# Attention outputs and blended tiles are split as they come, and one more feed-forward tile is computed plainly

## The chip, the cores and the metric

One Trainium2 chip, one core. The time is device microseconds of one execution. The kernel runs alone on its core; there are no collectives.

## What is computed

One inference step of a two-layer backbone for two groups of tokens that share all weights: 128 context tokens and 512 latent tokens, 640 in all, model width 1024. Cut to what the change touches, each layer is:

```python
h = rms_norm(x) * (1 + scale1) + shift1
z = h @ w_in                                  # conv streams, q, k, v, S5 input, three gates
y_attn = block_attention(q, k, v)             # 16 heads, 4 key/value heads
merged = sigmoid(g_conv) * (y_conv @ w_proj_conv) \
       + sigmoid(g_attn) * (y_attn @ w_proj_attn) \
       + sigmoid(g_ssm) * (y_ssm @ w_proj_ssm)
x = x + gate1 * (merged @ w_out)
h = rms_norm(x) * (1 + scale2) + shift2
x = x + gate2 * ((silu(h @ w_ffn_gate) * (h @ w_ffn_up)) @ w_ffn_down)   # width 2816
```

Scale, shift and gate come from an adaLN product with w_ada. All of it is float32 in and out.

## The kernel before

Activations lie transposed: a tile (`c2`) holds 128 channels of all 640 tokens, so a width of 1024 is 8 tiles. To keep float32 precision, each operand of a large product is split in a high half (a cast on ScalarE, to fp32r) and a low half (a subtraction on VectorE); `split` (L257) does it for activations and `halves` (L426) for weights. A product is then three terms, high-high, high-low and low-high, in two halves of 320 tokens: six matmuls of 320 columns for each of 8 k-tiles, 48 for an output tile (`gemm`, L844; `tile_gemm`, L982). `gemm` takes the k-tiles in order, so its matmuls wait for the split tiles one after the other.

Weights go through a ring of three raw tiles (`wr`), filled by DMAs on SP's queue in the order in which they are used, and three split tiles (`wh`). A converter runs at most two units ahead of the unit in use (`may`, L423). An adaLN unit (raw weights, no split) counts as one of these. `ada_n` (L319) says how many follow which tile: two after projection tile 0 ("pa", m=0), one after each of the others. What isn't converted when `w_get` (L488) asks for it is issued then, behind everything issued so far.

The program is written out by hand in one order for all engines. The main line is a generator (`layer`, L1895); beside it run side generators, for the attention seven of them. `pump` (L538) decides by a clock of its own, kept in Python while the program is written, which step comes next: a side step whose inputs are ready by the time the main line could go on is issued first. Each engine then runs its instructions in the order in which they were issued.

The attention works in four blocks b of four heads. `attn_out` (L1344) adds the outputs of block b into the two tiles ya[2b] and ya[2b+1]: eight products over the latent tokens (n = 0 to 7), then one over the context (n = 8), so both tiles of a block are complete only after its last product. While attention runs, the main line computes, in this order, q projections, gates, the GLU and the S5 branch, and the last gates (`gates`, L1934). Then `drain(att)` (L1946) issues the rest of the attention with nothing from the main line in between. All 8 ya tiles are split, and the projection runs: 8 tiles "pa", each evacuated by `blend` (L1017), two VectorE operations that multiply with the gate and add into merged[m]. After the eighth, all 8 merged tiles are split (L1952), x is reloaded from DRAM on SP's queue, and the 8 output tiles "o" follow, with `finish_x` (L1958) as evacuation.

PSUM has four tiles of two banks (`psb`). The pool of `c2` tiles has 57 (`NTILES`, L45). Counted in the program's order, from the first write of a tile to its last read, the most in use at once is 56, early in block b=2 of either layer.

The feed forward has 22 tiles of width 128 in five parts (`FF_PARTS`: 4, 4, 4, 5, 5). For each tile it needs a gate and an up product. Tiles below `PLAIN` take 2 x 48 matmuls. Those from `PLAIN` on are pairs (`glu_pair`, L906): a Strassen-Winograd scheme of seven quarter products, 7 x 12 = 84 matmuls, with sums of the weights made by two accumulating DMAs on POOL's queue and VectorE additions, and sums of h made by the side `sums` (L865) during the first tiles and by `quarters` (L890), which runs once, before the first pair. It makes four casts and four subtractions, half a tile wide each. After the tiles of a part comes its share of the down projection, 8 tiles of 24 matmuls (in the first four-tile part 192 in all), each added to x on VectorE by `gated`.

Of the kernel before, what the change touches and what calls it, by code (L numbers as in the profile page):

```python
# [17 lines left out]
KD = D // 128  # L18
# [13 lines left out]
GO = 0  # L32
# [13 lines left out]
WH = 3  # L46
RES = 1
FF_PARTS = ((0, 4), (4, 4), (8, 4), (12, 5), (17, 5))
PLAIN = 3
KS = (0, 4, 1, 5, 2, 6, 3, 7)  # L50
GQ = 4
GE = GQ * NCH
# [117 lines left out]
def trunk_kernel(ctx: ExitStack, tc: tile.TileContext, a):  # L170
    nc = tc.nc
    clk = Clock()
    pe, act, dve, sp, pool = (Engine(e, k, clk) for e, k in (
        (nc.tensor, "pe"), (nc.scalar, "act"), (nc.vector, "dve"), (nc.sync, "dma"), (nc.gpsimd, "pool")))
# [10 lines left out]
    def c2(dt=F32):  # L185
        return tp.tile([128, TK], dt, tag="c2", name="c2")
# [12 lines left out]
    def gps():  # L199
        t = bps()  # L200
        clk.held.add(t.name)
        clk.spare = 0
        return t

    def release(*ps):
        for t in ps:
            clk.held.discard(t.name)
# [7 lines left out]
    def f32(x):  # L215
        return x.bitcast(F32)
# [4 lines left out]
    def tt(out, in0, in1, op):  # L221
        dve.tensor_tensor(out=out, in0=in0, in1=in1, op=op)
# [4 lines left out]
    def add(out, x, y):  # L227
        tt(out, x, y, OP.add)

    def sub(out, x, y):  # L230
        tt(out, x, y, OP.subtract)
# [25 lines left out]
    def split(x):  # L257

        hi, lo = c2(F32R), c2(F32R)
        act.copy(hi, x)  # L260
        sub(lo, x, f32(hi))
        return hi, lo
# [56 lines left out]
    def ada_n(key):  # L319

        nm, l, m = key
        if nm == "pa":
            return 1 + int(m == 0)
        if nm == "fgu":
            return int(l == 0 and m < 14)
        if nm == "fd":
            return int(l == 0 and m in (4, 8))
        return int(nm == "o" and m < 7 - GO or l == 0 and (nm in ("cc", "cb") or nm == "fg" and m > 1))

    def tblk(key, *args):  # L330
        wblk(key, *args)
        ada_blk(ada_n(key))

    for l in range(DEPTH):
# [33 lines left out]
        for r0, nr in FF_PARTS:  # L368
            for m in range(r0, r0 + nr):
                if m < PLAIN:  # L370
                    tblk(("fg", l, m), a["w_ffn_gate"][l], 0, KD, 128 * m, 128)
# [116 lines left out]
    def w_get(key):  # L488
        u = wst["use"]
        assert units[u] == key, (units[u], key)  # L490
        wst["use"] += 1
        wst["used"] += 1 - wst["over"]
        wst["over"] = int(key[0] == "fgu" and key[3] == 3)
        while u not in wtile:
            cvt.step()
        return wtile.pop(u)
# [41 lines left out]
    def pump(need=(), until=None):  # L538

        own = [x for x in need if isinstance(x, str) and x in clk.t]  # L540
        m = clk.ready(need)
        while until is None or not until.done:
            if until is not None:
                m = INF
            elif not own:
                m = max(clk.ready(need), clk.t["pe"])
            t, x = min(((x.time(), x) for x in sides if not x.busy and not (x.prio == -1 and wst["hold"]) and (x.prio < 0 or not clk.calm)), key=lambda y: y[0], default=(INF, None))
            if t > m + SLACK or x is None or own and t == m and x.prio >= 0:
                return
            assert t < INF  # L550
            x.step()

    def drain(side):
        clk.spare = 0
        pump(until=side)
# [118 lines left out]
    def ada_pre(n):  # L674

        for l, v, q, kh in ada_gaps[:n]:
            w = []
            for j in range(2):
                t = c2()[:, 0:512].rearrange("p (k m) -> p k m", k=2)
                r0, c0 = 512 * kh + 256 * j, v * D + q * 256  # L680
                sp.dma_start(t, a["w_ada"][l][r0:r0 + 256, c0:c0 + 256].rearrange("(k p) m -> p k m", p=128))
                w += [t[:, 0, :], t[:, 1, :]]
            ada_w.append(w)
        del ada_gaps[:n]
# [159 lines left out]
    def gemm(ps, w, c0, acts, first=True, last=True, ks=None):  # L844

        K = len(acts)
        for i, k in enumerate(ks or range(K)):
            x = acts[k]
            if last and i >= K - RES:
                clk.spare = 1  # L850
            yield (w[0],) + x + (() if i else (ps,))
            for n, (r, s) in enumerate(((0, 0), (0, 1), (1, 0))):
                for h in range(2):
                    mm(ps[:, h, 0:HN], w[r][:, k, c0:c0 + 128], x[s][:, h * HN:(h + 1) * HN],
                       first and i == 0 and n == 0, last and i == K - 1 and n == 2)
# [116 lines left out]
    def v2(t):  # L972
        return t.rearrange("p (h n) -> p h n", h=2)
# [8 lines left out]
    def tile_gemm(key, acts, evac):  # L982
        w = w_get(key)
        ps = gps()
        yield from gemm(ps, w, 0, acts)
        evac(ps)
        release(ps)
        for _ in range(ada_n(key)):
            yield from ada_step()
# [27 lines left out]
    def blend(merged, m, th, ps):  # L1017

        stt(v2(th), v2(th), 1.0, pv2(ps), OP.add, OP.mult)
        if len(merged) <= m:  # L1020
            merged.append(th)
        else:
            add(merged[m], merged[m], th)
# [125 lines left out]
    class Attn:  # L1149
        pass  # L1150

    def attn_kv(l, A):
        A.cache = c2()
        for i, nm in enumerate(("cache_k", "cache_v")):
            sp.dma_start(A.cache[:, 256 * i:256 * i + 256], a[nm][0, l].rearrange("t h d -> t (h d)"))
        attn_tables(l)
        A.k, A.v = [], []
        yield from token_major(("k", l), A.hs, A.k)
# [182 lines left out]
            if PT:  # L1341
                pts.append(PT)

    def attn_out(preps, pts, done, ya):  # L1344

        for b in range(4):
            for n in range(9):
                yield lambda: len(pts) > done[4]
                vs, kp = preps[b][5], preps[b][4]
                PT = pts[done[4]]  # L1350
                yield PT[1], "b"
                ps = bps()
                if n < 8:
                    w = 256
                    prods = [(vs[:, 128 * k:128 * k + 128], PT[r][:, :, 128 * k:128 * k + 128])
                             for k in range(5) for r in range(2)]
                else:
                    w = 512
                    prods = [(kp[:, 256:384], PT[r][:, 0, 0:512]) for r in range(2)]
                for k, (v, p) in enumerate(prods):  # L1360
                    mm(ps[:, 0, 0:w], v, p, k == 0, k == len(prods) - 1)
                pts[done[4]] = None
                done[4] += 1
                clk.held.add(ps.name)
                yield ps, "act"
                u = c2()[0:64, 0:w]
                act.copy(u, ps[64:128, 0, 0:w])
                yield u,
                release(ps)
                if n < 8:  # L1370
                    r, c = 64 * (n // 2 % 2), 128 + 256 * (n % 2)
                    add(ya[2 * b + n // 4][r:r + 64, c:c + 256], ps[0:64, 0, 0:256], u)
                else:
                    for h in range(4):
                        r, c = 64 * (h % 2), slice(128 * h, 128 * h + 128)
                        add(ya[2 * b + h // 2][r:r + 64, 0:128], ps[0:64, 0, c], u[:, c])

    def attn_begin(l, A, raws, ya):
        preps, scores, exps, probs, turned, pts, done = [], [], [], [], [], [], [0] * 5
        out = Side(attn_out(preps, pts, done, ya), 0)  # L1380
        Side(attn_split(turned, pts, done), 0.1)
        Side(attn_turn(probs, turned, done), 0.2)
        Side(attn_norm(exps, probs), 0.5)
        Side(attn_exp(scores, exps), 0.7)
        Side(attn_scores(preps, scores, exps, done), 1)
        Side(attn_prep(l, A, raws, preps, done), 2)
        return out
# [507 lines left out]
    def layer(l, xs, stat, ssm):  # L1895
        up, ysT = ssm[1:]
        ssm = ssm[0]
        yc, merged = [], []
# [10 lines left out]
        merged = []  # L1909
        if l + 1 < DEPTH:  # L1910
            place_vecs(l + 1)
        A = Attn()
        A.hs, A.after = hs, ssm[1]
        yield from attn_kv(l, A)
        raws = []
# [3 lines left out]
            yield from token_major(("q", l, b), hs, raw)  # L1919
            raws.append(raw)  # L1920

        ya = [c2() for _ in range(KD)]
        att = attn_begin(l, A, raws, ya)
        v = []
        yield from token_major(("v", l), hs, v)
        A.v = v
# [5 lines left out]
        ths = []  # L1932
# [10 lines left out]
        ys = yield from glu(l, ysT)  # L1943
        yield from branch(l, "gs", "ps", hs, ys, merged)
        yield from gates(GA + GB, KD)
        drain(att)  # L1946
        ya = [split(y) for y in ya]
        for m in range(KD):
            yield from tile_gemm(("pa", l, m), ya, lambda ps: blend(merged, m, ths[m], ps))
            if m >= 8 - GO:  # L1950
                ada_pre(1)
        ms = [split(y) for y in merged]  # L1952
        ada_flush(l, 2)
        xs = reload_x()
        stat = []
# [20 lines left out]
        for part, (m0, nm) in enumerate(FF_PARTS):  # L1976
            hid = []
            tail = iter([0, 0, 0])
            for m in range(m0, m0 + nm):
                if m >= PLAIN:  # L1980
                    if x is None:
# [36 lines left out]
            for m in range(KD):  # L2018
# [4 lines left out]
                if m < 2:  # L2023
                    if m == 0:
                        two = yield from pair_ps(("fd", l, 0, m0), ("fd", l, 1, m0), hid)
                    ps = two[m]
                else:
                    ps = gps()
# [144 lines left out]
```

## Time and profile before

| | us |
|---|---|
| median of 3 runs | 2593.35 |
| lowest and highest | 2589.13, 2595.61 |
| the profiled execution | 2593.81 |
| its span | 2591.8 |

The profile is of one execution. Engines are PE (TensorE's matmuls), PEld (its weight loads, which overlap the matmuls), DVE (VectorE), ACT (ScalarE), POOL and SP (whose queue issues most DMAs). A matmul's recorded duration includes the time until its result has left the array, so matmuls of a stream overlap in the record; the pace is read from many of them in a row. All instructions are issued by one helper (L132), so rows are told apart by tiles: c is any activation tile, wh split weights, wr raw weights, pt the attention's probabilities or the pairs' weights, bps PSUM, ident the identity of a transpose. "[1.30 <-ACT c L132]" is the engine's idle time just before the instruction, and what ended it.

### The profile page before, as it was taken

Reading aid. Unit: us, or ns where it says so; the run is one execution under the profiler, and the core shown is the slowest. Engines: PE = TensorE matmul, PEld = TensorE weight load, DVE = VectorE, ACT = ScalarE, POOL = GpSimd, SP = SyncE. Lnnn points to the kernel's source line nnn. Section 1 sums busy time; section 2 is a strip of 40 time slices with the busy share of each in tenths; the row PEclk is TensorE's granted clock in tenths of the full one; section 3 lists DMA queues with packets and bytes.
Section 4 is the critical chain, followed back from the end, with each engine's and each line's share of the span. In section 5 each row is a group of like instructions: output and inputs, shape, how many; then the busy total and the mean of one; then the engine's idle time right before and its main releaser. Section 6 shows DMA issues by size and latency. Waiting matters only on the chain. (4 is left out here: it accounts for less than half of the span.)

```text
span 2591.8 us, 45359 instructions
## 1 busy us (share of the span) xinstructions
PE 2494.3 (96%) x18235; PEld 2398.9 (93%) x18235; DVE 1838.0 (71%) x3502; ACT 1155.5 (45%) x2096; POOL 97.9 (4%) x80
## 2 busy tenths in 40 slices
PE   6999999999999999999989999999998999999998
PEld 4899999999888899999979999899997889999998
DVE  5888787788744666675678887777887447766665
ACT  4343336556722533443443333365666225433443
POOL 0000000000000010111000000000000000111110
PEclk8999999999999999999989999999999999999999
DMA  9433331221037366665553233212110572565552
GB/s 267 139 106 114 96 96 51 64 67 42 17 114 237 92 144 141 147 145 128 122 167 94 78 99 117 63 44 86 52 45 24 175 201 58 118 143 123 114 125 72
DMA packets 465202, 280.46 MB, mean 108 GB/s; under 512 B 60184, under 2 KB 453216, under 8 KB 464992
## 3 DMA queue, kind: packets, MB, share of 16 engines
q1 hardware_dynamic: 424864, 257.63, 34.2%
q0 software_dynamic: 40128, 19.93, 6.2%
q8 instruction: 144, 2.36, 0.4%
q14 instruction: 66, 0.54, 0.1%
HBM read 257.37 MB, written 20.12 MB: 107 GB/s over the span
## 5 line engine op out<-in xcount | busy, mean ns | idle before, releaser
L132 PE MATMUL bps<-c,wh 128*128 128x320 f32 x11760 | 1822.7, 313 | 42.0 <-ACT c L132 20.7
L132 PEld LDWEIGHTS bps<-c,wh 128*128 128x128 f32 x11760 | 1745.3, 189 | 77.5 <-ACT c L132 25.8
L132 DVE TENSOR_TENSOR c<-c,c 128x512 f32<-128x512 f32 (+8 forms) x750 | 423.8, 592 | 57.9 <-ACT c L132 47.8
L132 ACT CAST wh<-wr 128x1024 fp32r<-128x1024 f32 (+2 forms) x286 | 267.9, 940 | 315.6 <-PE bps L132 157.7
L132 DVE TENSOR_TENSOR wh<-wr,wh 128x1024 fp32r<-128x1024 f32 (+2 forms) x286 | 309.3, 1086 | 129.7 <-ACT wh L132 128.6
L132 ACT COPY c<-bps 128x320 f32<-128x320 f32 (+7 forms) x363 | 150.7, 437 | 255.5 <-PE bps L132 250.8
L132 PE MATMUL bps<-c,c 128*128 128x320 f32 (+2 forms) x1416 | 234.8, 303 | 10.1 <-DVE c L132 6.5
L132 PEld LDWEIGHTS bps<-c,c 128*128 128x128 f32 x1416 | 204.4, 191 | 15.1 <-ACT c L132 10.4
L132 DVE TENSOR_TENSOR c<-c,bps 128x320 f32<-128x320 f32 (+1 forms) x222 | 125.0, 564 | 122.2 <-ACT c L132 106.4
L132 ACT ACTIVATE c<-c 128x640 f32<-128x640 f32 (+4 forms) x131 | 93.5, 722 | 210.2 <-DVE c L132 210.0
L132 PE MATMUL bps<-wh,c 128*128 128x256 f32 x1440 | 183.7, 286 | 2.9 <-ACT c L132 2.7
L132 PE MATMUL bps<-ident,c 128*128 128x128 f32 (+1 forms) x1115 | 159.2, 279 | 23.8 <-DVE c L132 9.9
L132 PEld LDWEIGHTS bps<-wh,c 128*128 128x128 f32 x1440 | 177.4, 193 | 3.8 <-ACT c L132 3.3
L132 ACT CAST c<-c 128x640 fp32r<-128x640 f32 (+3 forms) x192 | 113.4, 619 | 117.9 <-DVE c L132 116.8
L132 PEld LDWEIGHTS bps<-ident,c 128*128 128x128 f32 (+1 forms) x1115 | 131.1, 144 | 35.9 <-issue 10.2
L132 DVE SCALAR_TENSOR_TENSOR c<-bps,g2T,c 128x128 f32<-128x128 f32 (+2 forms) x240 | 89.7, 433 | 84.6 <-PE bps L132 84.6
L132 POOL DMA_DIRECT2D pt<-in_w_ffn_gate_dram x38 | 48.9, 1287 | 2344.8 <-DMA pt<-in_w_ffn_up_dram 2018.6
L132 DVE SCALAR_TENSOR_TENSOR c<-c,c 128x640 f32<-128x640 f32 (+3 forms) x124 | 102.8, 836 | 47.2 <-ACT c L132 45.4
L132 ACT ACTIVATE c<-bps,mx 128x640 f32<-128x640 f32 (+1 forms) x160 | 113.3, 712 | 36.4 <-DVE mx L132 35.7
L132 DVE TENSOR_REDUCE mx<-bps 128x1 f32<-128x640 f32 (+1 forms) x136 | 109.6, 809 | 27.8 <-PE bps L132 27.2
L132 ACT CAST wh<-pt 128x1024 fp32r<-128x1024 f32 x76 | 79.9, 1051 | 84.9 <-PE bps L132 83.7
L132 DVE TENSOR_TENSOR pt<-bps,pt 128x640 fp32r<-128x640 f32 (+1 forms) x136 | 109.4, 810 | 9.9 <-ACT pt L132 8.9
(105 smaller groups left out, 1541.2 us busy)
## 6 DMA issues: line engine op xcount, KB each, us to landing
wr<-in_w_in_dram SPq DMA_DIRECT2D x104, 512.0 KB
c<-in_w_ada_dram SPq DMA_DIRECT2D x110, 256.0 KB
wr<-in_w_ffn_gate_dram SPq DMA_DIRECT2D x44, 512.0 KB
wr<-in_w_ada_dram SPq DMA_DIRECT2D x41, 512.0 KB
pt<-in_w_ffn_up_dram SPq DMA_DIRECT2D x38, 512.0 KB
wr<-in_w_ffn_down_dram SPq DMA_DIRECT2D x48, 256.0 KB
wr<-in_w_ffn_down_dram SPq DMA_DIRECT2D x32, 320.0 KB
pt<-in_w_ffn_up_dram SPq DMA_DIRECT2D x38, 256.0 KB
```

Of the source, the lines that this page charges most:

```text
L132: res = f(*args, **kw)
```

## The change

`attn_out` splits the two tiles of a block as soon as the block is complete, and appends the halves to a list `yas`. This list, of the new class `Late`, says that it has 8 entries; when an entry is asked for that isn't there, the side generators are run until it is. `drain(att)` is gone: the projection begins at once, and `gemm` asks for one k-tile after the other. Each merged tile is split right after its own projection tile. `pump` takes a condition as well as a side to wait for. The `ada_pre` call that is dropped did nothing (GO is 0). `PLAIN` goes from 3 to 4: tile m=3 is computed plainly in both layers, so the whole first part is, and the first pair (and with it `quarters`) is m=4, after the first part's down projection.

```diff
--- before.py
+++ after.py
@@ -46,7 +46,7 @@
 WH = 3
 RES = 1
 FF_PARTS = ((0, 4), (4, 4), (8, 4), (12, 5), (17, 5))
-PLAIN = 3
+PLAIN = 4
 KS = (0, 4, 1, 5, 2, 6, 3, 7)
 GQ = 4
 GE = GQ * NCH
@@ -539,7 +539,8 @@
 
         own = [x for x in need if isinstance(x, str) and x in clk.t]
         m = clk.ready(need)
-        while until is None or not until.done:
+        over = (lambda: False) if until is None else until if callable(until) else lambda: until.done
+        while not over():
             if until is not None:
                 m = INF
             elif not own:
@@ -1148,6 +1149,19 @@
 
     class Attn:
         pass
+
+    class Late(list):
+
+
+        def __len__(self):
+            return KD
+
+        def __getitem__(self, k):
+            n = list.__len__
+            if n(self) <= k:
+                clk.spare = 0
+                pump(until=lambda: n(self) > k)
+            return list.__getitem__(self, k)
 
     def attn_kv(l, A):
         A.cache = c2()
@@ -1341,7 +1355,7 @@
             if PT:
                 pts.append(PT)
 
-    def attn_out(preps, pts, done, ya):
+    def attn_out(preps, pts, done, ya, yas):
 
         for b in range(4):
             for n in range(9):
@@ -1374,10 +1388,13 @@
                     for h in range(4):
                         r, c = 64 * (h % 2), slice(128 * h, 128 * h + 128)
                         add(ya[2 * b + h // 2][r:r + 64, 0:128], ps[0:64, 0, c], u[:, c])
-
-    def attn_begin(l, A, raws, ya):
+            for y in ya[2 * b:2 * b + 2]:
+                yield y, "act"
+                yas.append(split(y))
+
+    def attn_begin(l, A, raws, ya, yas):
         preps, scores, exps, probs, turned, pts, done = [], [], [], [], [], [], [0] * 5
-        out = Side(attn_out(preps, pts, done, ya), 0)
+        out = Side(attn_out(preps, pts, done, ya, yas), 0)
         Side(attn_split(turned, pts, done), 0.1)
         Side(attn_turn(probs, turned, done), 0.2)
         Side(attn_norm(exps, probs), 0.5)
@@ -1919,8 +1936,8 @@
             yield from token_major(("q", l, b), hs, raw)
             raws.append(raw)
 
-        ya = [c2() for _ in range(KD)]
-        att = attn_begin(l, A, raws, ya)
+        ya, yas = [c2() for _ in range(KD)], Late()
+        att = attn_begin(l, A, raws, ya, yas)
         v = []
         yield from token_major(("v", l), hs, v)
         A.v = v
@@ -1943,13 +1960,11 @@
         ys = yield from glu(l, ysT)
         yield from branch(l, "gs", "ps", hs, ys, merged)
         yield from gates(GA + GB, KD)
-        drain(att)
-        ya = [split(y) for y in ya]
+        ms = []
         for m in range(KD):
-            yield from tile_gemm(("pa", l, m), ya, lambda ps: blend(merged, m, ths[m], ps))
-            if m >= 8 - GO:
-                ada_pre(1)
-        ms = [split(y) for y in merged]
+            yield from tile_gemm(("pa", l, m), yas, lambda ps: blend(merged, m, ths[m], ps))
+            ms.append(split(merged[m]))
+            merged[m] = None
         ada_flush(l, 2)
         xs = reload_x()
         stat = []
```

## Rows read from the trace of the kernel before

**Rows 1.** Section 1 of the page: busy us, share of the span, instructions.

```profile
PE 2494.3 (96%) x18235; PEld 2398.9 (93%) x18235; DVE 1838.0 (71%) x3502; ACT 1155.5 (45%) x2096; POOL 97.9 (4%) x80
```

**Rows 2.** Who TensorE waited for, whole span: us in total, times, longest.

```profile
PE bps L132 <- DVE c L132: 33.6, 39, 4.2
```

**Rows 3.** Stretches: us, busy time of each engine (instructions), granted clock, DMA.

```profile
584.00:600.00 16.00, 16.00 (x117) 15.56 (x116) 11.76 (x24) 11.27 (x22) 0.00 (x0) 1.00 0.12 35
693.00:718.00 25.00, 18.69 (x120) 15.65 (x118) 19.18 (x40) 18.91 (x42) 0.00 (x0) 0.93 0.00 1
718.00:728.00 10.00, 9.42 (x62) 8.71 (x62) 6.49 (x9) 4.41 (x7) 0.00 (x0) 0.83 0.00 0
1937.00:1968.00 31.00, 31.00 (x230) 30.37 (x229) 21.12 (x43) 21.48 (x44) 0.00 (x0) 1.00 0.06 18
1968.00:1995.00 27.00, 20.93 (x145) 17.53 (x143) 22.63 (x46) 20.22 (x47) 0.00 (x0) 1.00 0.00 1
```

**Rows 4.** TensorE by line and shape, 1937 to 1968: busy us, mean ns, idle before.

```profile
L132 PE MATMUL bps<-c,wh 128*128 128x320 f32 x108 | 18.5, 314 | 0.0
```

**Rows 5.** Timeline, layer 0: start, us, engine, form, count, idle before.

```profile
716.48 1.19 DVE L132 TENSOR_TENSOR c<-bps,c 64x128 f32<-64x128 f32 x4 [0.41 <-ACT c L132]
...
718.58 8.55 PE L132 MATMUL bps<-c,wh 128*128 128x320 f32 x46 [0.90 <-DVE c L132]
...
727.06 1.07 PE L132 MATMUL bps<-wr,csT 128*32 128x256 f32 x16
```

**Rows 6.** Timeline, the same place in layer 1.

```profile
1993.92 5.12 ACT L132 CAST c<-c 128x640 fp32r<-128x640 f32 x8
1994.05 1.19 DVE L132 TENSOR_TENSOR c<-bps,c 64x128 f32<-64x128 f32 x4 [0.26 <-ACT c L132]
...
1996.16 7.01 PE L132 MATMUL bps<-c,wh 128*128 128x320 f32 x46 [0.90 <-DVE c L132]
...
2003.09 1.07 PE L132 MATMUL bps<-wr,csT 128*32 128x256 f32 x16
```

**Rows 7.** Timeline, projection tiles 0 to 2 of layer 0.

```profile
728.02 0.82 DVE L132 TENSOR_TENSOR c<-c,c 128x640 f32<-128x640 f32 x1
...
730.04 6.72 PE L132 MATMUL bps<-c,wh 128*128 128x320 f32 x44 [1.12 <-DVE wh L132]
...
737.26 7.30 PE L132 MATMUL bps<-c,wh 128*128 128x320 f32 x48
```

**Rows 8.** Timeline, first output tile: layer 0, then layer 1.

```profile
784.07 0.55 PE L132 MATMUL bps<-c,wh 128*128 128x320 f32 x2
...
786.08 7.01 PE L132 MATMUL bps<-c,wh 128*128 128x320 f32 x46 [1.46 <-DVE c L132]
...
2062.11 7.01 PE L132 MATMUL bps<-c,wh 128*128 128x320 f32 x46 [1.46 <-DVE c L132]
```

**Rows 9.** Timeline, feed forward m=2 and m=3: layer 0, then layer 1.

```profile
897.29 10.82 PE L132 MATMUL bps<-c,wh 128*128 128x320 f32 x72
...
922.20 0.64 PE L132 MATMUL bps<-c,csT 128*32 128x256 f32 x8
...
2178.74 4.56 PE L132 MATMUL bps<-c,wh 128*128 128x320 f32 x30
...
2180.68 3.42 ACT L132 CAST c<-c 128x640 fp32r<-128x640 f32 x7 [3.85 <-DVE c L132]
...
2185.42 2.65 PE L132 MATMUL bps<-c,wh 128*128 128x320 f32 x12 [2.12 <-ACT c L132]
...
2196.17 4.56 PE L132 MATMUL bps<-c,wh 128*128 128x320 f32 x30
```

**Rows 10.** Timeline, layer 1: down projection of part 0 and pair m=4.

```profile
2201.63 34.56 PE L132 MATMUL bps<-c,wh 128*128 128x320 f32 x234
...
2225.71 1.05 ACT L132 CAST wh<-pt 128x1024 fp32r<-128x1024 f32 x1 [2.47 <-PE bps L132]
2226.80 1.23 DVE L132 TENSOR_TENSOR wh<-pt,wh 128x1024 fp32r<-128x1024 f32 x1
```

## The prediction

> **What bounds the kernel now.** I read the busy shares first: TensorE is busy in 96% of the span [rows 1]. Then the list of who TensorE waited for; its longest entry, VectorE, is 33.6 us in all [rows 2]. So a change gains by fewer matmuls or in the gaps near the edited lines, and those I looked up. The table of stretches shows the first: while gates run beside the attention, TensorE is busy 31.00 of 31 us; when the gates have run out it is busy 18.69 of 25 us in layer 0 and 20.93 of 27 in layer 1, a tail that is a chain through VectorE (22.63 of 27) and ScalarE [rows 3]. The timelines show the others: projection 0 limping behind the splits of the attention outputs [rows 5, 6], projection 1 waiting for weights [rows 7], a wait in the first output tile [rows 8], a stall at the first Strassen pair, m=3 [rows 9]. The sum is made against the profiled execution, 2593.81 us (the span 2591.8 and 2.0 around it); the median shown is 0.46 lower, and I carry the difference over to it.
>
> **Pace.** 234 matmuls of 320 columns without a gap take 34.56 us [rows 10], 0.148 each; that price holds for all of them below. The Trainium skill, "TensorE: Matmul & The Clock Gate", section "Back-to-back issue gap", gives N/2.4 + 2.5 ns for an isolated matmul at full clock, 0.136 us here; by it the 24 matmuls that are added below would cost an estimated 3.3 us, not 3.6. The row decides.
>
> **Projection 0.** In layer 0 the attention's last additions end at 716.48 + 1.19 = 717.67, and the work after projection 0 starts at 727.06: 9.4 us [rows 5]. In layer 1 it is 1994.05 + 1.19 = 1995.24 to 2003.09, 7.85 us [rows 6]. The difference is the clock: 46 matmuls take 8.55 us against 7.01 [rows 5, 6], and the granted share is 0.83 in that stretch [rows 3], so TensorE ran part of it at 1.2 GHz, after a tail with idle time on and off. After the change the outputs of blocks 0 to 2 are split long before, so k = 0 to 5 (36 matmuls, 5.3 us) can go into the tail, which has 25 - 18.69 = 6.3 us idle, and 6.1 in layer 1 [rows 3]. Behind the last addition only y6 and y7 are left: casts of 0.64 (eight take 5.12 [rows 6]), subtractions of some 0.8 (0.82 for an addition of that shape [rows 7]), then six matmuls after the last one. The casts run beside the additions and subtractions: 0.2 + 2 x 0.75 + 0.9 = 2.6 us. Gain 6.8 and 5.25 us, if the attention ends when it did.
>
> It won't quite. In layer 1 VectorE's share is 21.12 / 31 = 0.68 in the mixed stretch and 22.63 / 27 = 0.84 in the tail [rows 3]; taken as the attention's speed, 108 matmuls of the gates [rows 4], 18 steps of six, set it back by 31 x (1 - 0.68/0.84) = 5.9 us, 0.33 a step, 2.0 us for six steps. The low end is 0 (VectorE is what is late in the tail, and its queue absorbs a step), the high end all of 5.3. Projection 0 also holds one of four PSUM tiles through the drain, where the attention had all four; part of that is in the 2.0, as a gate holds one too. I take 2.8: **+4.0 and +2.45**. Layer 0 has two dips of the clock (0.93 and 0.83 [rows 3]); a denser tail may lose one, the longer wait below may bring one: **+0.5**, -2 to +1.3 open.
>
> **The early splits**, 12 casts and 12 subtractions a layer, move to stretches where TensorE is fully busy and ScalarE has 21.48 of 31 us [rows 3]: nothing. Without that cover they'd cost what they cost now, at most the gains above.
>
> **Projection 1** waits already: after four matmuls 1.12 us for the low half of its weights [rows 7]. Two adaLN units follow projection 0 and the converter may not run that far ahead, so this subtraction is issued only when projection 1 asks for its weights, behind the blend's addition (728.02) on VectorE. The new split of merged[0] is issued just before that: on VectorE it stands in front of the weights' subtraction, and 44 matmuls wait behind. It waits for ScalarE's cast, 0.64 to 0.7 after the addition, some 0.1 for the semaphores, and then 0.82 of its own [rows 6, 7]: -1.6 a layer, **-3.2**. From m = 1 on one unit follows, weights come a tile ahead (48 matmuls in a row [rows 7]), and a split costs nothing: blend, split and weights are 3 x 0.82 + 1.23 = 3.7 us of VectorE in 7.3 [rows 7, 10].
>
> **First output tile.** Two matmuls at 784.07, the other 46 at 786.08, since the subtractions of all eight splits come after the last blend [rows 8]. After, seven are done long before, and the last (blend 2 x 0.82, cast 0.7, subtraction 0.82: 3.2 us) has seven k-steps, 6.2 us, as cover. Gain 2.01 - 0.30 = 1.7, and the same 1.46 us wait stands at 2062.11 [rows 8]: **+3.4**. The reload of x on SP's queue is issued at the same place, ahead of the 7 us of output tile 0 as before: nothing.
>
> **Feed forward, m=3.** As a pair it took, in layer 0, from 897.29 + 48 x 0.148 = 904.4 to 922.20, 17.8 us; in layer 1 from 2178.74 + 6 x 0.148 = 2179.6 to 2196.17, 16.5 us [rows 9]. Its 84 matmuls are 12.4 at the pace; the rest is a stall. In layer 1 the copy that frees the pair's bank stands on ScalarE behind seven casts that start at 2180.68, when m=2 is through; TensorE idles 2.12 us for it, and 12 matmuls then take 2.65 [rows 9]. Plain: 96 x 0.148 = 14.2 each. 34.3 - 28.4 = **+5.9**, with 3.6 for the 24 extra matmuls in it. Weights: two loads of 512 KB in the ring instead of three loads and two accumulating DMAs on POOL's queue; plain tiles follow one another without a gap now (72 in a row at 897.29 [rows 9]), so nothing. In layer 0 the adaLN unit of m=3 turns from two loads of its own on SP's queue into one in the weight ring; m=2 does that already ahead of those 72.
>
> The casts and subtractions of `quarters`, half as wide as a full tile, now stand before m=4, behind the down projection. ScalarE has just waited 2.47 us there [rows 10], so the casts cost nothing. The four subtractions (4 x 0.41 = 1.64) come on VectorE ahead of the weights' subtraction, which ends at 2226.80 + 1.23 = 2228.0; TensorE needs it 162 + 28 matmuls after 2201.63, at 2229.7 [rows 10]. 1.64 against 1.7 of slack: I take 0.3 a layer, **-0.6**; ends 0 and the old stalls, 5.4 and 4.1.
>
> **Room for tiles.** Counted in the program's own order from first write to last read, 56 of the 57 c2 tiles are in use early in block 2 (16 halves of h, 8 of the GLU, 8 merged, 5 ya, 2 gates, 17 others). Early splits add four halves and free two ya for each finished block: 60. Three tiles then wait for releases that come later, mostly on ScalarE. In 584 to 600, where block 2 begins, TensorE is busy 16.00 of 16 us and ScalarE 11.27 [rows 3], so ScalarE can lose some. No row shows such a wait; bounds 0 and rival 3. I take **-2.5**, nearer to 0 for that room.
>
> Sum: 6.45 + 0.5 - 3.2 + 3.4 + 5.9 - 0.6 - 2.5 = 9.95. 2593.81 - 9.95 = 2583.9; on the median **2583**.
>
> **Rivals.** (1) Paid back in the tail: each inserted matmul sets the attention back by its length, 5.3 instead of 2.8 in both layers, 5 us worse: **2588**. For it: TensorE's own part of the chain. Against: 6 us of idle per tail. (2) The stall moves with `quarters` to m=4, 9.5 instead of 0.6: **2592**. Against: ScalarE is idle there, and h was read long ago. (3) Too few tiles, slower: ScalarE is held early in block 2 and the attention stands for some 16 us (the GLU's 96 matmuls alone are 14). TensorE goes on with its gates, but those 16 us move into the tail, where 6.3 of 25 are idle [rows 3]: 4 us. ScalarE also evacuates the four GLU tiles in that stretch, and TensorE pays for a late one as at 2185.42, 2.12 us [rows 9]: 8.5. That is 12.5 a layer, 25 in all instead of 2.5: **2606**. It decides from some 20 us on (9.95 + 2.5 + 7.8). For it: 60 against 57. Against: ScalarE's free third. The Trainium skill, "Perfetto Trace Analysis", section "Optimization Strategy", says that the same gap repeating on an engine that should be saturated can mean too little SBUF or PSUM for the next tile; no run here shows it, and by it rival 3 would hold. (4) Nothing set back, no wait for tiles, both dips gone: 12.05 + 1.3 - 3.2 + 3.4 + 5.9 = 19.5, **2574**.
>
> **How the numbers follow.** Forecast (2578 to 2588) 0.47, rival 1 0.20, rival 2 0.10, rival 3 0.17, rival 4 0.06. The range, 2575 to 2598, takes in the first three, half of rival 4 and the milder third of rival 3. A measurement tells some 0.3% (7.8 us) from no change. Faster, below 2585.6: four fifths of the forecast, rival 4, a quarter of rival 1, 0.49. Slower, above 2601: most of rival 3, 0.16. Same: 0.35.
>
> **What would show it.** Right: steps of six projection matmuls between the attention's last transposes; some 2.6 us from the last addition to the end of projection 0; at projection 1 four matmuls and then 2.7 us of wait for VectorE; no gap in the first output tile; m=2 and m=3 in a row, and under 0.5 us of gap at m=4. Wrong: the last addition over 5 us later after the last gate (rival 1), an m=4 pair of over 14 us (rival 2), gaps on TensorE in block 2 with ScalarE waiting (rival 3).

## The result: 20.6 us slower

The changed kernel takes 2612.59 us (median of four runs, 2608.21 to 2614.32) against 2592.01 for the kernel before beside it: ratio 1.0076, interval 1.0058 to 1.0095. Forecast were 2583 and a range of 2575 to 2598. The profiled execution of after has a span of 2612.6 us.

The page of after, section 1 (busy us, share of the span, instructions), answers [rows 1]:

```profile
PE 2500.5 (96%) x18259; PEld 2405.2 (92%) x18259; DVE 1830.9 (70%) x3486; ACT 1149.7 (44%) x2084; POOL 92.8 (4%) x76
```

The list of who TensorE waited for in after (us in total, times, longest) answers [rows 2]:

```profile
PE bps L132 <- ACT c L132: 37.4, 24, 5.7
PE bps L132 <- DVE c L132: 26.2, 33, 4.2
PE bps L132 <- DVE wh L132: 10.5, 11, 2.7
PE bps L132 <- DVE pt L132: 8.9, 11, 1.2
```

The same entries of before, beside the one in [rows 2]:

```profile
PE bps L132 <- ACT c L132: 31.8, 28, 5.7
PE bps L132 <- DVE wh L132: 7.4, 9, 1.4
...
PE bps L132 <- DVE pt L132: 2.2, 5, 0.6
```

TensorE is busy 6.2 us longer; the other 14.6 us of the span are waits. The wait for VectorE's activation tiles, which the change aimed at, fell from 33.6 to 26.2 us. But the forecast read that one entry as VectorE in all. With the entries for weights (wh) and probabilities (pt), the waits for VectorE went from 43.2 to 45.6 us, and the wait for ScalarE's tiles from 31.8 to 37.4: they moved, and grew. To see where the time went, take points that both programs have and compare their times:

| point | before | after | later by |
|---|---|---|---|
| an adaLN row step, ahead of every edit | 200.4 | 203.3 | 2.9 |
| layer 0, end of attention block 0, where the orders part | 505.2 | 506.0 | 0.8 |
| layer 0, end of projection 0 | 727.06 | 732.48 | 5.4 |
| end of projection 1 | 736.69 | 743.72 | 7.0 |
| end of the first output tile | 793.02 | 798.34 | 5.3 |
| end of the third output tile | 808.62 | 818.58 | 10.0 |
| end of the pair m=4 | 964.34 | 970.66 | 6.3 |
| layer 1, an adaLN row step at its start | 1345.2 | 1353.1 | 7.9 |
| end of attention block 0 | 1780.1 | 1787.0 | 6.9 |
| end of projection 0 | 2003.09 | 2020.52 | 17.4 |
| end of the third output tile | 2084.65 | 2106.61 | 22.0 |
| end of the pair m=4 | 2237.79 | 2258.64 | 20.9 |

The first two differences lie ahead of every edit and are the spread of single executions: from 475 to 490 us, for one, the granted clock is 0.77 in before and 0.89 in after, so each ran part of that at 1.2 GHz, and before more of it. What is left has three main places: the attention from the end of block 0 to the end of projection 0 (4.65 us lost in layer 0, 10.56 in layer 1, where 4.0 and 2.45 were forecast as gains), the third output tile (4.6 and 3.1 lost, not forecast), and the feed forward (3.6 and 1.1 gained from one line of the table to the next; in layer 1, 1.6 us lost ahead of it at a lower clock hide the rest). Projection 1 loses 1.6 and 3.1 us, and the first output tile gains 1.7 in each layer.

Stretches of after (us; busy time and instructions of PE, PEld, DVE, ACT, POOL; granted clock; DMA share and GB/s), for [rows 3]:

```profile
584.00:600.00 16.00, 13.61 (x93) 13.24 (x92) 10.25 (x21) 8.25 (x16) 0.00 (x0) 0.97 0.23 67
...
693.00:718.00 25.00, 19.81 (x146) 17.94 (x144) 19.77 (x38) 17.86 (x39) 0.00 (x0) 1.00 0.01 2
718.00:733.00 15.00, 10.62 (x68) 8.61 (x72) 9.47 (x20) 9.18 (x21) 0.00 (x0) 0.89 0.00 0
```

Early in block 2 ScalarE is busy 8.25 us, not 11.27, and TensorE has gaps. The attention stands there, as rival 3 said. At the other end it is still at work at 718 to 728, where it had finished before.

The last gate's matmuls in layer 0 (timeline), in after:

```profile
683.00 1.04 PE L132 MATMUL bps<-c,wh 128*128 128x320 f32 x6
```

And in before:

```profile
691.01 1.92 PE L132 MATMUL bps<-c,wh 128*128 128x320 f32 x12
```

From their end to the attention's last addition it takes 44.5 us (684.04 to 728.56), where it took 24.7 (692.93 to 717.67); in layer 1 it takes 48.0 instead of 27.6. The forecast had named a last addition over 5 us later after the last gate as the sign of rival 1. The 36 early matmuls of projection 0 stand there in steps of six, as forecast.

The end of the attention in after (timeline: start, us, engine, form, count, idle before and its releaser), layer 0 and layer 1, for [rows 5, 6]:

```profile
727.37 1.19 DVE L132 TENSOR_TENSOR c<-bps,c 64x128 f32<-64x128 f32 x4 [0.26 <-ACT c L132]
728.76 3.79 PE L132 MATMUL bps<-c,wh 128*128 128x320 f32 x12 [2.04 <-ACT c L132]
732.48 1.07 PE L132 MATMUL bps<-wr,csT 128*32 128x256 f32 x16
...
2016.01 1.19 DVE L132 TENSOR_TENSOR c<-bps,c 64x128 f32<-64x128 f32 x4 [0.65 <-ACT c L132]
2018.25 2.33 PE L132 MATMUL bps<-c,wh 128*128 128x320 f32 x10 [0.30 <-DVE c L132]
2020.52 1.94 PE L132 MATMUL bps<-wr,csT 128*32 128x256 f32 x16
```

From the last addition to the work after projection 0: 732.48 - 728.56 = 3.9 us and 2020.52 - 2017.20 = 3.3 us, where 9.4 and 7.85 stood before. 2.6 was forecast; in layer 0 the last twelve matmuls ran at 1.2 GHz for the most part (3.79 us where twelve in before took 1.92; granted clock 0.89 in the stretch). So the step behind the last addition went nearly as forecast. But the last addition itself came at 728.56 instead of 717.67, and at 2017.20 instead of 1995.24.

The projections and the output tiles of layer 0 in after, for [rows 7, 8]:

```profile
733.45 0.82 DVE L132 TENSOR_TENSOR c<-c,c 128x640 f32<-128x640 f32 x1
735.06 0.82 DVE L132 TENSOR_TENSOR c<-c,c 128x640 fp32r<-128x640 f32 x1 [0.79 <-ACT c L132]
735.80 1.22 DVE L132 TENSOR_TENSOR wh<-wr,wh 128x1024 fp32r<-128x1024 f32 x1
737.08 6.71 PE L132 MATMUL bps<-c,wh 128*128 128x320 f32 x44 [2.74 <-DVE wh L132]
...
791.11 7.30 PE L132 MATMUL bps<-c,wh 128*128 128x320 f32 x48
...
807.41 0.74 ACT L132 ACTIVATE c<-c 128x640 f32<-128x640 f32 x1 [7.06 <-DVE c L132]
808.06 1.03 ACT L132 CAST wh<-wr 128x1024 fp32r<-128x1024 f32 x1
809.14 0.85 PE L132 MATMUL bps<-c,wh 128*128 128x320 f32 x4 [2.36 <-ACT wh L132]
810.39 8.25 PE L132 MATMUL bps<-c,wh 128*128 128x320 f32 x44 [0.41 <-DVE wh L132]
```

Projection 1 waits 2.74 us instead of 1.12, and the first three lines show why: the subtraction of the blended tile stands between the blend and the weights. The first output tile runs without a gap. The third one waits: on ScalarE its weights' cast (808.06) stands behind the square of the second tile (807.41), which waits for that tile's last addition. In before the cast stood ahead of that square (timeline of before):

```profile
797.55 1.05 ACT L132 CAST wh<-wr 128x1024 fp32r<-128x1024 f32 x1 [2.52 <-DMA wr<-in_w_out_dram]
802.10 0.74 ACT L132 ACTIVATE c<-c 128x640 f32<-128x640 f32 x1 [3.50 <-DVE c L132]
```

The feed forward of after, both layers, for [rows 9, 10]:

```profile
907.22 14.35 PE L132 MATMUL bps<-c,wh 128*128 128x320 f32 x96
...
932.65 36.32 PE L132 MATMUL bps<-c,wh 128*128 128x320 f32 x246
968.80 1.92 PE L132 MATMUL bps<-c,c 128*128 128x320 f32 x12
...
2160.42 59.66 PE L132 MATMUL bps<-c,wh 128*128 128x320 f32 x400 [0.30 <-DVE c L132]
...
2220.72 36.32 PE L132 MATMUL bps<-c,wh 128*128 128x320 f32 x246
```

Matmuls in a row, at the pace of before, and no gap at m=4.

### The profile page after: what moved, and what is told of

The parts are those of the page before. It is cut to its first block, busy times and chain, and to the rows that moved or that the text cites. A ratio compares the mean times of both kernels' runs of the same rounds, so it can differ in the third digit from the quotient of the medians.

```text
span 2612.6 us, 45384 instructions
## 1 busy us (share of the span) xinstructions
PE 2500.5 (96%) x18259; PEld 2405.2 (92%) x18259; DVE 1830.9 (70%) x3486; ACT 1149.7 (44%) x2084; POOL 92.8 (4%) x76
## 5 line engine op out<-in xcount | busy, mean ns | idle before, releaser
L132 DVE TENSOR_TENSOR c<-c,c 128x512 f32<-128x512 f32 (+7 forms) x750 | 425.8, 591 | 70.4 <-ACT c L132 60.3
L132 ACT COPY c<-bps 128x320 f32<-128x320 f32 (+8 forms) x355 | 147.3, 437 | 237.2 <-PE bps L132 233.2
L132 PEld LDWEIGHTS bps<-c,c 128*128 128x128 f32 x1392 | 200.4, 191 | 23.1 <-ACT c L132 14.7
L132 DVE SCALAR_TENSOR_TENSOR c<-c,bps 128x640 f32<-128x640 f32 (+1 forms) x72 | 53.6, 745 | 84.5 <-PE bps L132 69.0
```

The costliest lines, as they stand in the source:

```text
L132: res = f(*args, **kw)
```

## The experiments

Every run stands beside runs of the kernel before on the same chip.

| run | us | before | ratio, interval |
|---|---|---|---|
| late | 2603.03 | 2592.98 | 1.0036, 1.0024 to 1.0049 |
| order_only | 2618.12 | 2592.98 | 1.0098, 1.0083 to 1.0112 |
| old_order | 2602.26 | 2592.98 | 1.0038, 1.0026 to 1.0050 |
| ms_only | 2603.37 | 2592.98 | 1.0040, 1.0028 to 1.0052 |
| ff_only | 2584.80 | 2591.18 | 0.9977, 0.9968 to 0.9986 |
| ms_fix | 2588.17 | 2591.18 | 0.9988, 0.9980 to 0.9997 |
| tail_only | 2596.23 | 2591.18 | 1.0025, 1.0016 to 1.0034 |
| best | 2583.61 | 2591.18 | 0.9974, 0.9963 to 0.9984 |
| tail_early | 2598.71 | 2591.23 | 1.0027, 1.0017 to 1.0038 |
| tail_end | 2592.68 | 2591.23 | 1.0006, 0.9997 to 1.0015 |
| best2 | 2584.95 | 2591.23 | 0.9975, 0.9966 to 0.9985 |
| best3 | 2585.99 | 2591.28 | 0.9978, 0.9967 to 0.9989 |

### Early splits: the order or the tiles?

After has less attention work early in block 2. Two theories: casts that wait for a free tile hold ScalarE (rival 3); or the planner, which lays out all engines' work by clocks of its own, lays it out differently once the splits stand in it. Counted in the programs, 92 score matmuls (queries with keys) of layer 0 stand among the 432 matmuls with weights that follow block 0's end in before, and 72 in after: an order, fixed before anything runs. Three kernels tell the theories apart; by the same count late and old_order have the 92 of before, and order_only the 72 of after.

**late**, the control: the blocks done by then are split when the gates end.

```diff
-                yield y, "act"
-                yas.append(split(y))
+                if yas.go:
+                    yield y, "act"
+                    yas.append(split(y))
+                else:
+                    yas.late.append(y)
...
         yield from gates(GA + GB, KD)
+        yas.extend(split(y) for y in yas.late)
+        yas.go = True
```

> The changed kernel, but the outputs of every block that is done when the gates end are split there, all at once, and not as they come; projection 0 still begins in the tail. Up to the end of layer 0's gates the program's order is that of the kernel before. Theory A (the early splits are what cost: 2.6 us lost in layer 0 and 9.5 in layer 1 by the end of projection 0, where 4.0 and 2.45 were to be gained): most of the 18.5 us comes back, less 2 to 4 us a layer for six splits at once on VectorE in the tail: 2596, between 2590 and 2602. Theory B (beginning projection 0 in the tail costs, its steps of six and its PSUM tile set the attention back): nothing comes back, 2608 to 2615.

**order_only**: late, with the planner's clocks moved on as if the early splits were there.

```diff
                 else:
+                    yield y, "act"
+                    clk.op("act", 633.0, ["hi" + y.name], [y.name])
+                    clk.op("dve", 737.0, ["lo" + y.name], [y.name, "hi" + y.name])
                     yas.late.append(y)
```

> The changed kernel with its own order of all other instructions up to layer 0's gates' end (the planner is told of early splits), but without them: the outputs of blocks 0 to 2 are split when the gates end, as in the run late. No tile is asked for earlier than in the kernel before, and no cast or subtraction stands in block 1 or 2. Theory A1 (the planner's order is what costs: it issues gates where it issued attention before, so the attention reaches the tail some 12 us behind): as the changed kernel or a little worse for the six splits in the tail, 2610 to 2620. Theory A2 (rival 3 of the forecast: waits for tiles cost): as late, some 2596.

**old_order**: late, with real splits of blocks 0 and 2 that the planner doesn't see.

```diff
+                elif b in (0, 2):
+                    hi, lo = c2(F32R), c2(F32R)
+                    nc.scalar.copy(hi, y)
+                    nc.vector.tensor_tensor(out=lo, in0=y, in1=f32(hi), op=OP.subtract)
+                    yas.late.append((hi, lo))
```

> The run late with the splits of blocks 0 and 2 put in as soon as the block ends, without the planner's knowledge, so that all other instructions keep the order of the kernel before; block 1 is split when the gates end. Casts, subtractions and the early demand for tiles are there (58 of 57 live at the peak, one has to wait), the new order is not. A1 (order): 0 to 4 us faster than late, since four splits leave the tail: about 2593. A2 (tiles): more than 5 us slower than late, 2602 to 2610.

Measured: late +10.05 us against before, order_only +25.14, old_order +9.28. late lies 1 us outside its theory A and well below theory B, so beginning projection 0 in the tail costs something too (next section). The order alone costs 15.1 us with not one early split in the program; early splits of blocks 0 and 2 in the old order cost nothing on balance against late, which has them in the tail. TensorE by shape from 560 to 620 us (busy us, mean ns, idle before), in after:

```profile
L132 PE MATMUL bps<-c,wh 128*128 128x320 f32 x258 | 42.5, 316 | 0.9 <-DVE c L132 0.9
L132 PE MATMUL bps<-c,c 128*128 128x320 f32 x28 | 6.2, 347 | 2.4 <-ACT c L132 2.4
```

The same view of late:

```profile
L132 PE MATMUL bps<-c,wh 128*128 128x320 f32 x245 | 40.0, 312 | 0.0
L132 PE MATMUL bps<-c,c 128*128 128x320 f32 x48 | 9.4, 318 | 0.0
```

And of order_only:

```profile
L132 PE MATMUL bps<-c,wh 128*128 128x320 f32 x269 | 43.2, 312 | 0.9 <-DVE c L132 0.9
L132 PE MATMUL bps<-c,c 128*128 128x320 f32 x36 | 7.0, 316 | 0.1
```

Where late does 48 score matmuls, after does 28 and order_only 36, and both do more matmuls with weights instead. TensorE stays busy, so the stretch looks harmless; the price comes in the tail, when the weights' matmuls have run out and the attention is left: from the last gate to the last addition of layer 0 order_only takes 52.5 us and late 32.8.

The tiles do play a part, a small one. Timeline of after, a place that comes once a layer:

```profile
597.89 0.82 DVE L132 TENSOR_TENSOR c<-c,c 128x640 f32<-128x640 f32 x1
598.75 0.58 ACT L132 CAST c<-bps 128x512 fp32r<-128x512 f32 x1 [3.20 <-DVE c L132]
599.38 1.44 PE L132 MATMUL bps<-c,c 128*128 128x320 f32 x4 [2.39 <-ACT c L132]
```

The cast reads nothing that this addition (a blend's) writes; but it writes a new tile, and the addition is the last reader of one. Counted in the program, 58 of 57 tiles are wanted at that peak. Layer 1 has the same 2.39 us at 1884.62, and order_only, which asks for no tile early, has neither gap. That is 4.8 us for both layers. The demand alone doesn't make the gap: old_order wants 58 tiles too, by the same count, and has no wait of that size early in block 2. After is all the same 4.6 us better than order_only. Its splits are gone from the tail, which from the last gate to the last addition takes 44.5 and 48.0 us instead of 52.5 and 53.0; no run shows that apart. Splitting each of the three blocks at its own end in the old order was not tried.

### Projection 0 in the tail

**tail_only**: before with nothing but projection 0 begun in the tail, and the blocks done by then split when the gates end, as in late. **tail_early**: the same, with the splits of blocks 0 to 2 put into the mixed stretch, unseen by the planner (block 0 at its end, 1 and 2 at the end of block 2). **tail_end**: tail_early, with projection 0 begun when the attention's last matmuls are issued.

At a block's end, in both:

```diff
+            for c in ((0,), (), (1, 2), ())[b]:
+                for y in yas.late[2 * c:2 * c + 2]:
+                    hi, lo = c2(F32R), c2(F32R)
+                    nc.scalar.copy(hi, y)
+                    nc.vector.tensor_tensor(out=lo, in0=y, in1=f32(hi), op=OP.subtract)
+                    yas.append((hi, lo))
```

Ahead of projection 0, in tail_end alone:

```diff
+        clk.spare = 0
+        pump(until=lambda: yas.done[4] >= 36)
```

> The kernel before with projection 0 begun in the tail, the outputs of the blocks done by then split when the gates end (as in the run late), and nothing else of the change. By late less ms_only less the gain of the feed forward, 2603.0 - 10.4 + 6.3: 2598.9, that is some 6 us slower than before: each inserted matmul sets the attention back by its length and the six splits come on top (rival 1, worse than it was priced). By the forecast's step (6.45 gained) it would be 2586.5, and then late's loss lies in how the parts meet.

> The run tail_only (5.05 us slower than before), but no split is left for the tail but that of y6 and y7: block 0 is split at its own end, blocks 1 and 2 at the end of block 2, outside the planner, so that the order of everything else up to the gates' end is that of before in layer 0. If the inserted matmuls of projection 0 are what sets the attention back (rival 1): at most 1.5 us faster than tail_only, as old_order was 0.8 faster than late: 2595. If the twelve casts and subtractions in the tail were the cost: 5 us a layer back, 2586.

> The run tail_early, but projection 0 begins only when the attention's last matmuls are issued: its first 36 matmuls stand on TensorE behind those, beside the last copies, additions and splits, and none among the attention's steps. In layer 1 of before the last attention matmuls end at 1993.4 and the work after projection 0 starts at 2003.09, 9.7 us; now 36 matmuls (5.3) and 12 (1.8): 7.1, so 2.6 us gained a layer, and the clock of layer 0's projection open. If the place of the matmuls is what costs in tail_only: 2591.2 - 5.2 = 2586, some 10 us faster than tail_only. If something else in the edit costs (the early casts, the held PSUM tile): 2591 or more.

Measured: +5.05, +7.48 and +1.45 us. So beginning projection 0 at the gates' end costs 5 us where 6.45 was to be gained, and on balance it doesn't help to take the splits out of the tail. Layer 1 of tail_only, whose order up to the gates' end is that of before, shows the mechanism (timeline):

```profile
1969.97 5.25 PE L132 MATMUL bps<-c,wh 128*128 128x320 f32 x34 [0.30 <-DVE c L132]
1975.06 0.71 PE L132 MATMUL bps<-ident,c 128*128 128x128 f32 x5
...
1998.61 1.93 PE L132 MATMUL bps<-pt,c 128*128 128x256 f32 x12
...
2003.44 1.73 PE L132 MATMUL bps<-c,wh 128*128 128x320 f32 x10 [0.30 <-DVE c L132]
2005.11 1.07 PE L132 MATMUL bps<-wr,csT 128*32 128x256 f32 x16
```

The attention's last matmuls stand at 1998.6 instead of 1991.6: 36 matmuls (5.3 us) were put in, and it came 7.0 us later. From there to the end of projection 0 it takes 6.5 us instead of 11.5. Seven lost, five gained. Here the matmuls stand in one row behind the splits, and the transposes behind that row, at 1968.58 in before, are late by 6.5 us already.

Not all of the seven is the matmuls: six casts and six subtractions stand in that tail too. tail_early and tail_end differ only in where projection 0 stands, and neither has these splits in its tail. From the end of the last gate's matmuls to the last addition, tail_early takes 26.2 us in layer 0 and 32.4 in layer 1, tail_end 23.4 and 27.7. So the 36 matmuls by themselves, in steps of six, set the attention back by 2.7 and 4.8 us. In tail_only, against before, it is 8.0 and 7.0.

In tail_end the place of the attention is kept, and projection 0 ends at 2000.17 instead of 2003.09 in layer 1 and at 721.61 instead of 727.06 in layer 0. Counted from the last gate, that is a gain of 2.7 and 5.6 us; part of the 5.6 is the clock, since it runs at full clock where before ran partly at 1.2 GHz. Timeline of tail_end, layer 1:

```profile
1993.05 7.19 PE L132 MATMUL bps<-c,wh 128*128 128x320 f32 x48
2000.17 1.07 PE L132 MATMUL bps<-wr,csT 128*32 128x256 f32 x16
```

So the place of the matmuls costs, 6 us between tail_early and tail_end. Yet tail_end gains nothing over before, because the early splits cost as much ahead of the tail. From the end of block 0 (its last addition) to the end of the last gate, with the same matmuls in the same order, it takes 191.6 us in layer 0 and 192.2 in layer 1 (tail_early the same), where before takes 187.7 and 187.5: 3.9 and 4.7 us. In layer 1 the largest piece lies at the end of block 2, where the four splits stand together (timeline of tail_end):

```profile
1938.66 2.62 ACT L1400 CAST c<-c 128x640 fp32r<-128x640 f32 x4
1939.78 3.03 DVE L1401 TENSOR_TENSOR c<-c,c 128x640 fp32r<-128x640 f32 x4
1943.27 0.77 PE L132 MATMUL bps<-ident,c 128*128 128x128 f32 x5 [1.86 <-DVE c L132]
1944.98 0.85 PE L132 MATMUL bps<-c,c 128*128 128x320 f32 x4 [0.94 <-ACT c L132]
```

In before VectorE is idle for a third of such a stretch [rows 3], and TensorE stands 2.8 us all the same: its queue is in order, the attention's transposes wait for VectorE there, and the gates stand behind them.

### The other two parts, and a better kernel

**ms_only**: before, with the split of each blended tile right behind its blend. **ms_fix**: the same one tile later, and the converter let on ahead of an output tile's epilogue.

In ms_only:

```diff
+            ms.append(split(merged[m]))
-        ms = [split(y) for y in merged]
```

In ms_fix:

```diff
+            if m:
+                ms.append(split(merged[m - 1]))
+        ms.append(split(merged[KD - 1]))
...
-            yield from tile_gemm(("o", l, m), ms, lambda ps: finish_x(m, ps, g1T[l]))
+            yield from tile_gemm(("o", l, m), ms, lambda ps: (advance(9), finish_x(m, ps, g1T[l])))
```

> The kernel before, and of the change only the split of the blended tiles as they come. By the forecast: 1.6 us lost a layer at projection 1, 1.7 gained at the first output tile, 2592. If the stall that the changed kernel shows at the third output tile (4 matmuls, 2.4 us of wait for ScalarE's weight cast) comes from this part: 2.9 us lost a layer on top, 2598; if it comes from the later end of the attention, no stall there and 2592.

> The run ms_only with its two orders put right: a blended tile is split one tile later than it is blended, so that its subtraction no longer stands ahead of projection 1's weights; and an output tile's epilogue first lets the converter go on, so that the third tile's weights are cast ahead of the second tile's square. If the two waits (1.62 and 2.9 us a layer) and the clock that falls behind them are all that ms_only lost, only the gain at the first output tile is left, 3.4 us: 2589.5, between 2587 and 2592. If something else cost there: 2595 or more.

Measured: +10.39 and -3.01 us. Timeline of ms_only, layer 0:

```profile
726.40 8.25 PE L132 MATMUL bps<-c,wh 128*128 128x320 f32 x44 [2.74 <-DVE wh L132]
...
799.99 0.85 PE L132 MATMUL bps<-c,wh 128*128 128x320 f32 x4 [2.36 <-ACT wh L132]
801.25 6.71 PE L132 MATMUL bps<-c,wh 128*128 128x320 f32 x44 [0.41 <-DVE wh L132]
```

Both waits come from this part alone, and 44 matmuls after the 2.74 us take 8.25 instead of 6.72 us. Summed over both layers: 2 x 1.62 at projection 1, 2 x 1.53 of clock behind it, 2 x 3.1 at the third output tile and 0.8 of clock there in layer 1, less 3.4 at the first output tile: 9.9, near the 10.39. With the two orders put right nearly the whole gain is left; in layer 0 of ms_fix the third output tile still takes 1.0 us longer than in before.

**ff_only** is before with PLAIN = 4, **best** is ff_only and ms_fix, **best2** is best with tail_end, and **best3** spreads best2's early splits over the attention's steps, a cast at one and its subtraction at the next.

> The kernel before with the m=3 of the feed forward plain, and nothing else of the change. The forecast gave it 5.9 less 0.6: 2587.7. The changed kernel's trace shows 3.6 us gained in layer 0 and 2.7 in layer 1 by the end of the pair m=4, and no wait there: 2586.7. If the stall had only moved to m=4 (rival 2): 2592 to 2593.

> ff_only and ms_fix together, without the early splits and without a projection begun in the tail. If the gains add: 2593.0 - 6.3 - 3.4 = 2583.3, between 2581 and 2587.

> The run best (2583.6) with tail_end's projection 0. If the gains add: 2583.6 - 5.2 = 2578.4, between 2576 and 2583.

> The run best2 (2585.0), but the splits of blocks 0 to 2 no longer stand four at a time at the end of block 2: one cast is put into the attention's outputs every third step of the next block and its subtraction a step later, outside the planner. In the trace of tail_end the four together held VectorE for 3.0 us and ScalarE for 2.6, and TensorE stood 1.86 and 0.94 us behind them in layer 1, where 4.7 us were lost from the layer's start to the end of the gates. If the burst is the cost: best (2583.6) less the 5.2 us gained at projection 0, 2578, between 2576 and 2581. If VectorE and ScalarE have no room for the splits in any place there: 2583 to 2586.

Measured: -6.38, -7.57, -6.28 and -5.29 us. The feed forward holds what was expected; best is the lowest, within the interval of ff_only: its two gains, 9.4 by themselves, add up to 7.6. Neither best2 nor best3 is faster; both lie above what was expected if the gains added. In best3 TensorE is busy 39.69 us from 1920 to 1960 against 37.19 in best2, so the burst is gone, and the time is not better. The way from the end of block 0 to the last gate shows why: it takes 191.5 and 191.2 us in best3, 191.6 and 192.2 in best2, and 187.7 and 187.5 in best, which has no early splits. Spread out, the splits cost nearly as much as in a burst. That is the other outcome named for best3, no room for them in any of these places; how small waits add up to that is open.

The sum for the change: feed forward -6.4, blended tiles +10.4, projection begun in the tail +5.05, and early splits, after against late, 20.6 - 10.05 = +10.5 (the order +15.1, the rest -4.6). Together 19.6 of 20.6 us; what is missing is late's, 10.05 against the 9.1 of its three parts.

## Why the prediction was wrong

1. **The early splits, "nothing", is the step that failed worst.** It put the casts and subtractions (six of each a layer; the 12 of each that it counts are those of both layers) into the old program and asked whether the engines have room. But the planner lays out the whole program again around them; attention moved behind gates, and that alone costs 15.1 us. The step was blind to an effect of the first order in a kernel whose order is computed. Its other half, room on ScalarE and VectorE, fell too: in the old order, in tail_end, the splits made the way to the last gate 3.9 and 4.7 us longer, and one burst of four held TensorE 2.8 us.
2. **Projection 0, +4.0 and +2.45, had the wrong sign.** The 2.6 us behind the last addition came out as 3.9 and 3.3, near enough. The setback by the matmuls, forecast as 2.8, was 2.7 us in layer 0 of tail_early and 4.8 in layer 1, there nearly rival 1's 5.3. What the step left out is the splits that it needs: in the tail, with the matmuls in a row behind them, they bring the setback to 8.0 and 7.0 us (tail_only); ahead of it they cost 3.9 and 4.7. The idle 6 us of the tail are not free for the taking: they are waits inside a chain, and TensorE is a link of it.
3. **The third output tile** was not in the sum: 3.1 us a layer, and 1.5 of clock in layer 0. The forecast weighed SP's queue at this place and not ScalarE's, where the weights' cast fell behind a square.
4. **Room for tiles, -2.5**, was half its size: 4.8 us, by one wait a layer. The program wants 58 tiles at its peak, not 60. Rival 3 named the symptom (attention standing in block 2, gaps, a longer tail) and the nearest time, 2606; its mechanism made a quarter of it. The Trainium skill, "Perfetto Trace Analysis", section "Optimization Strategy", says that the same gap repeating for a stretch on the engine that should be saturated can mean too little room for the next tile. The gap of 2.39 us does come from a missing tile, but it stands once a layer and not for a stretch, and the larger loss has no such gap.
5. **Right:** projection 1 (1.62 us more wait, 1.6 forecast; the clock behind it was left out), the first output tile (1.7 gained), the feed forward (6.4 against 5.9 less 0.6: no stall at m=4, so rival 2 is out).
6. **The clock, +0.5**, was too kind. Several stretches behind new waits ran partly at 1.2 GHz, some 1.5 us each.

## What to carry to other kernels

When a planner orders the program, an edit's price is the price of the new order: compare the two orders before costing the instructions, and to test one part, keep the old order and put the instruction in unseen. Idle time in a tail that one chain sets is little room for other work on an engine of that chain; put the work behind the chain's last instruction there. Idle time of VectorE and ScalarE isn't free either, where TensorE's next instruction waits for them. And for every instruction moved, ask on each engine what it now stands in front of.

## What the hardware showed that I had not expected

Waits of 2 to 3 us on TensorE can cost more than their length. Behind the 1.12 us of wait at projection 1 of before, 44 matmuls take 6.72 us; behind the 2.74 us in ms_only they take 8.25, with a granted clock of 0.88 over 721 to 735, so part of them ran at 1.2 GHz. Not each time: in after, 44 matmuls behind 2.74 us took 6.71 at projection 1 of layer 0, and 8.25 at the third output tile.
